# Fifty-three weight chunks of a float32 decoder block brought in and split by two GpSimd DMAs each, with the low-part matmuls moved behind the high-part ones

## The chip, the cores and the metric

The kernel runs on one core of one Trainium2 chip. The metric is the device time of one execution in microseconds. The trace is one profiled execution; times in it count from the start of its span. TensorE's clock has two levels, 1.2 and 2.4 GHz, and the profile shows the granted one as a share of the higher.

## What is computed

One decoder layer on 512 tokens of 1024 columns, in float32. The reference, cut to what matters here:

```python
h = rms_norm(x, g_norm1) * (1.0 + sc1) + sh1
z = h @ w_in                       # 8 kinds of columns, split below
(gu, gv, mq, mk, mv, mo, mi, mf, nq, nkc, nvc, nks, nvs, nkw, nvw, ngate, ga, gbr, gc) = split(z)
y_a = gmlp_mixer(gu, gv, ...) @ w_up_a
y_b = mlstm_mixer(mq, mk, mv, mo, mi, mf, ...) @ w_up_b
y_c = nsa_mixer(nq, nkc, nvc, nks, nvs, nkw, nvw, ngate, ...) @ w_up_c
x = x + gt1 * ((sigmoid(ga) * y_a + sigmoid(gbr) * y_b + sigmoid(gc) * y_c) @ w_out)
h = rms_norm(x, g_norm2) * (1.0 + sc2) + sh2
x = x + gt2 * (square(relu(h @ w_mlp1)) @ w_mlp2)
return rms_norm(x, g_final)
```

`sh1`, `sc1` and the other four rows of the modulation come from `silu(c) @ w_ada + b_ada`.

## The kernel before

Float32 products are made of float32r parts: a value is a high part (rounded to float32r) plus a low part (the rest), and each product takes three matmuls: high with high, low activations with high weights, high activations with low weights (`mm3`). The activations h^T stay in SBUF as eight pairs `hh[k]`, `hl[k]`. The weights come in chunks of 128 x 1024 (some 768, 864 or 576 columns wide). For each chunk, `chunk()` does three things: SyncE loads a tile `w_raw` (three buffers), ScalarE copies it rounded into `w_hi`, and an engine subtracts: `w_lo = w_raw - w_hi`. `w_hi` and `w_lo` have two buffers each, so chunk n+2 takes the tiles of chunk n. With `pool_lo=True` GpSimd does the subtraction, otherwise VectorE. GpSimd has 53 chunks: 8 of `w_early` (the first GEMM, six column tiles of q and k, one chunk for each block k), 2 of `w_zt` (compressed keys and values), 3 of `w_small`, 12 in `early_fill` (beside the attention loop), 24 in the gated merges of branches 2 and 0, and 4 in `fill_og`. The chunks of the conv, of merge 1 and of everything after them are VectorE's.

The stages in order of time: a start that loads x and makes the norm and the modulation of the first sub-layer (`early_mod`, `early_h`: VectorE and GpSimd multiply the transposed rows of `w_ada` by the condition, tile `ada_raw`, line L207 on GpSimd and L210 on VectorE), with the first GEMM running along it, one chunk per block; the two `zt` tiles and the three `sm` chunks; the attention loop with `early_fill` between its steps; the merges with the conv and the mLSTM heads; then the rest of the modulation, the output projection and the MLP.

What sets the order: each engine runs its own instructions in program order and waits there. In the first GEMM the order on TensorE is as written, in the attention loop that on TensorE, ScalarE and VectorE is; elsewhere, and always on GpSimd and on SyncE's DMA queue, a scheduler fixes the order when the program is built. The loop of the first GEMM, the same in both kernels, is this (c0 to c7 below are its eight chunks):

```python
            for i in range(6):
                T.matmul(early[i], wh[:, tsl(i)], hh[j], start=j == 0, stop=False)
            ...
            for i in range(6):
                T.matmul(early[i], wh[:, tsl(i)], hl[j], start=False, stop=False)
                T.matmul(early[i], wl[:, tsl(i)], hh[j], start=False, stop=j == KD - 1)
```

The functions that the change touches:

Of the kernel before, what the change touches and what calls it, by code (L numbers as in the profile page):

```python
# [11 lines left out]
ALU = mybir.AluOpType  # L12
# [48 lines left out]
def trunk_kernel(ctx: ExitStack, tc: tile.TileContext, x, vecs, rows, late_rows, ada1, w_ada,  # L61
# [15 lines left out]
    def page(tag, name, dt=F32, width=S):  # L77
        """a tile of 512 columns (and a little) that outlives the step that writes it"""
        t = work.tile([P, 520 if tag == "kv" else S], dt, name=name, tag=tag, bufs=SLOTS[tag])
        return t[:, :width]  # L80
# [10 lines left out]
    def split(hi, lo, src, scale=None):  # L91
        """src (times scale) as the exact sum of two float32r parts"""
        if scale is None:
            A.copy(hi, src)
            V.tensor_tensor(lo, src, f(hi), op=ALU.subtract)
        else:
            A.activation(hi, src, AF.Copy, scale=scale)
            V.scalar_tensor_tensor(lo, src, scale, f(hi), op0=ALU.mult, op1=ALU.subtract)
# [6 lines left out]
    def chunk(src, cols=D, pool_lo=False, dve_hi=False):  # L105
        raw = load(src, cols)
        hi = stream.tile([P, D], F32R, name="w_hi", tag="hi")[:, :cols]
        lo = stream.tile([P, D], F32R, name="w_lo", tag="lo")[:, :cols]
        V.tensor_copy(hi, raw) if dve_hi else A.copy(hi, raw)  # L109
        (G if pool_lo else V).tensor_tensor(lo, raw, f(hi), op=ALU.subtract)  # L110
        return hi, lo
# [5 lines left out]

    def rstd_of(ss, n, name, scale=1.0 / D):
        """1/sqrt(ss*scale + EPS)"""
        r = small.tile([P, n], F32, name=name)  # L120
        V.tensor_scalar(r, ss, scale, EPS, op0=ALU.mult, op1=ALU.add)
        G.tensor_tensor(r, r, mhalf[:, 0:r.shape[1]], op=ALU.pow)
        return r
# [4 lines left out]
    # ---------------------------------------------------------------- loads and constants of the start  # L128
# [24 lines left out]
    # the condition as a row on all partitions  # L153
# [7 lines left out]
    # ---------------------------------------------------------------- first norm, transposed and split  # L161
# [20 lines left out]
    # 1/rms of the tokens as a row on all partitions  # L182
# [9 lines left out]
    def early_mod(j):  # L192
        """shift and scale of a column tile: the first by the tensor engine, the others along rows of the
        transposed weights"""
# [61 lines left out]
    # ---------------------------------------------------------------- constants of the mixers  # L256
# [23 lines left out]
    # ---------------------------------------------------------------- GEMM helpers on h^T  # L280
    def zt(n, pool_lo=False, tag="mm"):
        """column tile n of z, transposed: [128 columns, S]"""
        wh, wl = chunk(w_zt[n], D, pool_lo)
        ps = bank(tag, "zt")
        for k in range(KD):
            mm3(ps, wh[:, tsl(k)], wl[:, tsl(k)], hh[k], hl[k], k == 0, k == KD - 1)
        return ps

    def ztok(n, evac, pool_lo=True):
        """256 columns of z in token layout: two banks of two blocks; a step for each chunk of weights"""  # L290
        ps = [bank("mm", "ztok") for _ in range(2)]
        for c in range(2):
            wh, wl = chunk(w_tok[n * 2 + c], D, pool_lo)
            for tb in range(NT):
                o = ps[tb // 2][:, (tb % 2) * 256:(tb % 2) * 256 + 256]
                for kk in range(4):
                    k = 4 * c + kk
                    ws_ = slice(kk * 256, (kk + 1) * 256)
                    T.matmul(o, hh[k][:, tsl(tb)], wh[:, ws_], start=k == 0 and tb % 2 == 0, stop=False)
                    T.matmul(o, hl[k][:, tsl(tb)], wh[:, ws_], start=False, stop=False)  # L300
                    T.matmul(o, hh[k][:, tsl(tb)], wl[:, ws_], start=False, stop=k == KD - 1 and tb % 2 == 1)
# [6 lines left out]
    # ---------------------------------------------------------------- NSA operands  # L308
# [32 lines left out]
    # compressed keys and values: the windows, gathered by pairs of positions  # L341
    vc = []
    # per group: 32 columns of the high parts, 32 of the low ones
# [20 lines left out]
    def halves(name, src, eng):  # L364
        """16 blocks of 64 columns, each beside its rest: both float32r parts in one operand of 128 columns"""
# [42 lines left out]
    # values of the two dense branches, mLSTM gates, NSA gates: token layout  # L408
# [6 lines left out]
    for c, (k0, k1) in enumerate(((0, 3), (3, 6), (6, 8))):  # L415
        wh, wl = chunk(w_small[:, k0 * 288:k1 * 288], (k1 - k0) * 288, pool_lo=True)
        for tb in range(NT):
            for k in range(k0, k1):
                ws_ = slice((k - k0) * 288, (k - k0 + 1) * 288)
                T.matmul(sm[tb][:, :288], hh[k][:, tsl(tb)], wh[:, ws_], start=k == 0, stop=False)  # L420
                T.matmul(sm[tb][:, :288], hl[k][:, tsl(tb)], wh[:, ws_], start=False, stop=False)
                T.matmul(sm[tb][:, :288], hh[k][:, tsl(tb)], wl[:, ws_], start=False, stop=k == KD - 1)
# [11 lines left out]
    # ---------------------------------------------------------------- NSA attention  # L434
# [4 lines left out]
    def cmp_scores(g):  # L439
        """scores and weights of the compressed branch for the four heads of group g, in steps"""  # L440
# [43 lines left out]
    def scores(n, tb):  # L484
        """a block of rows of the scores, their bias and their maximum"""
# [24 lines left out]
    def scale(n, t0, t1):  # L510
        """exp(s - max) of blocks t0 to t1 times gate / sum"""
# [10 lines left out]
    def turn(n, sb):  # L522
        """the weights of a block of keys, transposed"""
# [14 lines left out]
    def apply(n, sb):  # L538
        """values of a block of keys times their weights"""
# [32 lines left out]
    # ---------------------------------------------------------------- gMLP  # L572
# [12 lines left out]
    def gelu2(ts):  # L585
        """twice the gelu, in place"""
# [54 lines left out]
    def mlstm_gates():  # L641
# [23 lines left out]
        # sums of the log forget gates within blocks of 128, the running stabilizer  # L665
# [37 lines left out]
    def evac_mv(half):  # L703
        def ev(tb, ps):
            # two heads to a page: high part, one, zero, low part
# [14 lines left out]
    def conv(i, ps):  # L720
        """column tile i of q and k after the conv, silu and scale: two float32r parts"""
# [99 lines left out]
    # ---------------------------------------------------------------- merge of the gated branches  # L821
# [3 lines left out]
    def merge(b, yh, yl):  # L825
        """adds branch b of the three, two column tiles at a time: gates, then the projection up"""
        for jp in range(4):
# [8 lines left out]
            wh, wl = chunk(w_up[b][jp], D, pool_lo)  # L836
            for u in range(2):
                j = 2 * jp + u
                ps = bank(UP_BANK[b][u], "up")
                for k in range(4):  # L840
                    mm3(ps, wh[:, tsl(u * 4 + k)], wl[:, tsl(u * 4 + k)], yh[k], yl[k], k == 0, k == 3)
# [12 lines left out]
    # ---------------------------------------------------------------- mixers beside the GEMMs  # L854
    def early_fill():
        """the first GEMMs on h^T in small steps, with the weights of the next chunk under way"""
# [7 lines left out]
        for m, (kind, i) in enumerate(units):  # L864
# [3 lines left out]
            if kind == "z":  # L868
                ps = bank("mm", "zt")
                for k in range(KD):  # L870
                    mm3(ps, wh[:, tsl(k)], wl[:, tsl(k)], hh[k], hl[k], k == 0, k == KD - 1)
                    if k < KD - 1:
# [8 lines left out]
            for tb in range(NT):  # L881
                o = ps[tb // 2][:, (tb % 2) * 256:(tb % 2) * 256 + 256]
                for kk in range(4):
                    k = 4 * c + kk
                    ws_ = slice(kk * 256, (kk + 1) * 256)
                    T.matmul(o, hh[k][:, tsl(tb)], wh[:, ws_], start=k == 0 and tb % 2 == 0, stop=False)  # L886
                    T.matmul(o, hl[k][:, tsl(tb)], wh[:, ws_], start=False, stop=False)  # L887
                    T.matmul(o, hh[k][:, tsl(tb)], wl[:, ws_], start=False, stop=k == KD - 1 and tb % 2 == 1)
                    if kk == 1 or (kk == 3 and (c == 0 or tb % 2 == 0)):
                        yield  # L890
                if c == 1 and tb % 2 == 1:
                    ev = (evac_gv(0), evac_gv(1), evac_mv(0), evac_mv(1))[n]
                    for t_ in (tb - 1, tb):
                        ev(t_, ps[t_ // 2][:, (t_ % 2) * 256:(t_ % 2) * 256 + 256])
                    yield
# [68 lines left out]
    # row sums of the masked weights carry the bias of the norm  # L964
# [38 lines left out]
    # ---------------------------------------------------------------- the rest of the modulation  # L1003
# [58 lines left out]
    # ---------------------------------------------------------------- output projection, second norm  # L1062
# [14 lines left out]
    def tok_gemm(chunks, ah, al, finish, tags, held=None, between=None, tail=None):  # L1077
        """sum over k of ah/al[k]^T times two blocks of weight rows per chunk, in token layout; with pages for the
        last chunks (held) the blocks finish one after the other"""
# [17 lines left out]
        def half_step(u, k, wh, wl):  # L1097
            """the last block of tokens, half of the columns"""
# [108 lines left out]
    # ---------------------------------------------------------------- MLP  # L1207
# [15 lines left out]
    def final_half(ps, u, us):  # L1223
        """the last block, half of its last columns at a time"""
# [24 lines left out]
    def relu2(n, ps):  # L1249
        """relu squared, split"""  # L1250
# [32 lines left out]
def _layout(inp):  # L1283
# [7 lines left out]
    def tiles_t(w):  # L1291
        """[K, N] -> [N/128, 128, K] : column tile, row in its block, (block, column)"""
# [3 lines left out]
    def tiles_k(w):  # L1296
        """[K, N] -> [N/512 * K/256, 128, 1024] : half, pair of row blocks"""
# [60 lines left out]
```

## Time and profile before

| What | Value |
|---|---|
| Times of three runs | 972.73, 973.5, 974.67 us (median 973.5) |
| Span of the profiled execution | 973.2 us |
| TensorE busy | 933.4 us, 96% |
| VectorE busy | 612.2 us, 63% |
| ScalarE busy | 402.4 us, 41% |
| GpSimd busy | 193.7 us, 20% |
| DMA | 111.72 MB, 115 GB/s on average |

The profiled execution has no time apart from its span; the span lies 0.3 us under the median. TensorE's busy time counts overlapping matmuls once, and a matmul of 512 columns that shows 0.39 us of its own starts 0.23 us after the one before it, so "busy" does not mean that no faster pace is possible, but idle time of TensorE is real idle time.

### The profile page before, as it was taken

The numbers are of one execution on the slowest core, as the hardware profiler recorded it, in microseconds if no ns is written. First come the engines' busy times: TensorE is split into PE (matmuls) and PEld (weight loads), VectorE is DVE, ScalarE is ACT, GpSimd is POOL, SyncE is SP. The second block draws the span as 40 slices with busy tenths as digits, with TensorE's granted clock in tenths as the row PEclk, the third lists the DMA queues.
The fourth block names the chain that finished last, engine by engine and source line by source line (L and its number), as shares of the span: only waits on it lengthen the run. The fifth ranks groups of instructions, "written<-read, shape, count | busy, mean of one in ns | idle before, by whom it ended". The sixth has DMA issues, their size and how long they took to land.

```text
span 973.2 us, 12531 instructions
## 1 busy us (share of the span) xinstructions
PE 933.4 (96%) x4688; PEld 778.5 (80%) x4688; DVE 612.2 (63%) x1186; ACT 402.4 (41%) x789; POOL 193.7 (20%) x130
## 2 busy tenths in 40 slices
PE   7789998998979999999999999999999999999996
PEld 5569986797867888888977778888888888888886
DVE  6977679776497456556688799766424254442435
ACT  5355565765533444443333344544321223432221
POOL 5565423333343122123300003000000000000001
PEclk9899999998999999999999999999999999999998
DMA  9733210110222222222568864354333333223222
GB/s 328 229 118 116 66 44 26 40 44 26 84 65 87 87 86 88 70 82 89 172 211 274 258 251 119 92 182 128 94 100 91 104 89 107 87 89 106 87 87 87
DMA packets 36285, 111.72 MB, mean 115 GB/s; under 512 B 4160, under 2 KB 4352, under 8 KB 36224
## 3 DMA queue, kind: packets, MB, share of 16 engines
q1 hardware_dynamic: 36224, 110.91, 35.0%
q8 instruction: 37, 0.61, 0.3%
q14 instruction: 24, 0.20, 0.1%
HBM read 108.80 MB, written 2.10 MB: 114 GB/s over the span
## 4 chain that ended last, share of the span: by engine, by line
PE 75%; DVE 15%; DMA 6%; issue 2%; ACT 1%; SPq 0%; POOL 0%; POOLq 0%; DVEq 0%; ACTq 0%
PE tok L1086 6%; PE tok L1088 6%; PE tok L1087 6%; PE m L114 6%; PE m L116 6%; PE m L115 6%; PE zt L116 5%; PE zt L114 5%; PE zt L115 5%; DMA ada_raw<-in_w_ada 4%; DVE ada_raw L210 2%; PE pv L553 2%; PE pT L528 2%; PE ztok L887 2%; PE ztok L886 2%
## 5 line engine op out<-in xcount | busy, mean ns | idle before, releaser
L109 ACT CAST w_hi<-w_raw 128x1024 fp32r<-128x1024 f32 (+2 forms) x137 | 141.4, 1032 | 256.6 <-PE tok L1087 98.0
L110 DVE TENSOR_TENSOR w_lo<-w_raw,w_hi 128x1024 fp32r<-128x1024 f32 x84 | 103.8, 1236 | 171.1 <-ACT w_hi L109 171.1
L110 POOL TENSOR_TENSOR w_lo<-w_raw,w_hi 128x1024 fp32r<-128x1024 f32 (+3 forms) x53 | 125.1, 2360 | 242.9 <-ACT w_hi L109 240.3
L116 PE MATMUL zt<-h_hi,w_lo 128*128 128x512 f32 x304 | 121.1, 398 | 4.0 <-POOL w_lo L110 2.3
L114 PE MATMUL zt<-h_hi,w_hi 128*128 128x512 f32 x304 | 122.3, 402 | 0.5 <-ACT w_hi L109 0.5
L115 PE MATMUL zt<-h_lo,w_hi 128*128 128x512 f32 x304 | 119.9, 394 | 0.0
L114 PE MATMUL m<-h_hi,w_hi 128*128 128x512 f32 (+1 forms) x272 | 104.1, 383 | 0.0
L116 PE MATMUL m<-h_hi,w_lo 128*128 128x512 f32 (+1 forms) x272 | 103.7, 381 | 0.0
L115 PE MATMUL m<-h_lo,w_hi 128*128 128x512 f32 (+1 forms) x272 | 103.6, 381 | 0.0
L1087 PE MATMUL tok<-w_hi,f_lo 128*128 128x512 f32 (+1 forms) x232 | 88.6, 382 | 0.0
L1086 PE MATMUL tok<-w_hi,f_hi 128*128 128x512 f32 (+1 forms) x232 | 88.6, 382 | 0.0
L1088 PE MATMUL tok<-w_lo,f_hi 128*128 128x512 f32 (+1 forms) x232 | 84.4, 382 | 0.0
L116 PEld LDWEIGHTS zt<-h_hi,w_lo 128*128 128x128 f32 x304 | 57.6, 190 | 17.3 <-DVE w_lo L110 2.8
L114 PEld LDWEIGHTS zt<-h_hi,w_hi 128*128 128x128 f32 x304 | 57.6, 189 | 12.1 <-ACT w_hi L109 0.7
L115 PEld LDWEIGHTS zt<-h_lo,w_hi 128*128 128x128 f32 x304 | 57.6, 190 | 10.7
L1228 POOL TENSOR_TENSOR o_g<-x,gfin 128x512 f32<-128x512 f32 x1 | 1.3, 1297 | 311.0 <-DVE x L1132 311.0
L115 PEld LDWEIGHTS m<-h_lo,w_hi 128*128 128x128 f32 x272 | 51.2, 188 | 10.8
L116 PEld LDWEIGHTS m<-h_hi,w_lo 128*128 128x128 f32 x272 | 51.1, 188 | 10.8
L114 PEld LDWEIGHTS m<-h_hi,w_hi 128*128 128x128 f32 x272 | 51.1, 188 | 10.7
L1087 PEld LDWEIGHTS tok<-w_hi,f_lo 128*128 128x128 f32 x232 | 43.6, 188 | 8.6
L1086 PEld LDWEIGHTS tok<-w_hi,f_hi 128*128 128x128 f32 x232 | 43.6, 188 | 8.5
L1088 PEld LDWEIGHTS tok<-w_lo,f_hi 128*128 128x128 f32 x232 | 43.6, 188 | 8.4
(390 smaller groups left out, 2022.3 us busy)
## 6 DMA issues: line engine op xcount, KB each, us to landing
w_raw<-in_w_m SPq DMA_DIRECT2D x64, 512.0 KB, 3.5
w_raw<-in_w_zt SPq DMA_DIRECT2D x38, 512.0 KB, 3.3
ada_raw<-in_w_ada SPq DMA_DIRECT2D x24, 512.0 KB, 5.1
ada_raw<-in_ada SPq DMA_DIRECT2D x32, 256.0 KB, 4.9
w_raw<-in_w_tok SPq DMA_DIRECT2D x12, 512.0 KB, 3.3
w_raw<-in_w_up SPq DMA_DIRECT2D x12, 512.0 KB, 3.5
w_raw<-in_w_out SPq DMA_DIRECT2D x8, 512.0 KB, 4.8
w_raw<-in_w_ada SPq DMA_DIRECT2D x8, 512.0 KB, 3.9
```

The lines of the kernel that those rows point to most:

```text
L109: V.tensor_copy(hi, raw) if dve_hi else A.copy(hi, raw)
L110: (G if pool_lo else V).tensor_tensor(lo, raw, f(hi), op=ALU.subtract)
L114: T.matmul(ps, ah, bh, start=first, stop=False)
L115: T.matmul(ps, ah, bl, start=False, stop=False)
L116: T.matmul(ps, al, bh, start=False, stop=last)
L210: V.scalar_tensor_tensor(raws[q], raws[q], 1.0, condb[:, (q % 2) * 512:(q % 2) * 512 + 512], op0=ALU.mult, op1=ALU.mult, accum_out=s4[:, q ...
L528: T.transpose(tp[:, tsl(tb)], sb_[:, boff(tb) + c0:boff(tb) + c0 + P], ident)
L553: T.matmul(acc[:, c0:], vv, p_[:, c0:], start=False, stop=last and p_ is t[-1])
L886: T.matmul(o, hh[k][:, tsl(tb)], wh[:, ws_], start=k == 0 and tb % 2 == 0, stop=False)
L1086: T.matmul(p_, ah_, wh, start=k == 0, stop=False)
L1087: T.matmul(p_, al_, wh, start=False, stop=False)
L1088: T.matmul(p_, ah_, wl, start=False, stop=k == 2 * n - 1)
```

## The change

For the 53 chunks with `pool_lo`, `w_raw`, ScalarE's copy and GpSimd's subtraction go. GpSimd issues a DMA from HBM straight into `w_hi`, which rounds on the way. ScalarE writes the negative of `w_hi` into `w_lo`. GpSimd then issues a second DMA of the same weights, which adds them to `w_lo`. Outside the first GEMM the matmuls that read `w_lo` move behind all that read `w_hi` of the same chunk. The core of the diff:

```diff
     def chunk(src, cols=D, pool_lo=False, dve_hi=False):
-        raw = load(src, cols)
         hi = stream.tile([P, D], F32R, name="w_hi", tag="hi")[:, :cols]
         lo = stream.tile([P, D], F32R, name="w_lo", tag="lo")[:, :cols]
+        if pool_lo:
+            G.dma_start(hi, src)
+            A.activation(lo, f(hi), AF.Copy, scale=-1.0)
+            G.dma_start(lo, src, accum_op=ALU.add)
+            return hi, lo
+        raw = load(src, cols)
         V.tensor_copy(hi, raw) if dve_hi else A.copy(hi, raw)
-        (G if pool_lo else V).tensor_tensor(lo, raw, f(hi), op=ALU.subtract)
+        V.tensor_tensor(lo, raw, f(hi), op=ALU.subtract)
         return hi, lo
...
+    def mm_hi(ps, ah, bh, bl, first):
+        T.matmul(ps, ah, bh, start=first, stop=False)
+        T.matmul(ps, ah, bl, start=False, stop=False)
...
         for k in range(KD):
-            mm3(ps, wh[:, tsl(k)], wl[:, tsl(k)], hh[k], hl[k], k == 0, k == KD - 1)
+            mm_hi(ps, wh[:, tsl(k)], hh[k], hl[k], k == 0)
+        for k in range(KD):
+            T.matmul(ps, wl[:, tsl(k)], hh[k], start=False, stop=k == KD - 1)
...
```

`ztok`, the `sm` loop, `early_fill` and the projections up in `merge` are split in the same way (16 or 32 matmuls on the high tile, then 8 or 16 on the low one); `merge` opens both of its two banks before the first low matmul.

In the rows that follow, line numbers are those of each kernel's own file. GpSimd's queue, in the first GEMM, before. `w_lo_268` is the low tile of c1, `w_lo_317` of c2, and so on; the `ada_raw` rows are the modulation's:

```order
L207 TENSOR_TENSOR ada_raw_259<-ada_raw_259,condb_119 128x512
L110 TENSOR_TENSOR w_lo_268<-w_raw_265,w_hi_267 128x768
L207 TENSOR_TENSOR ada_raw_308<-ada_raw_308,condb_119 128x512
L110 TENSOR_TENSOR w_lo_317<-w_raw_314,w_hi_316 128x768
L207 TENSOR_TENSOR ada_raw_357<-ada_raw_357,condb_119 128x512
L110 TENSOR_TENSOR w_lo_366<-w_raw_363,w_hi_365 128x768
```

The same queue after the change. `w_hi_312` and `w_lo_313` belong to c2, 360 and 361 to c3, 408 and 409 to c4, 456 to c5:

```order
L110 DMA w_hi_312<-in_w_early 128x768
L218 TENSOR_TENSOR ada_raw_354<-ada_raw_354,condb_119 128x512
L110 DMA w_hi_360<-in_w_early 128x768
L218 TENSOR_TENSOR ada_raw_402<-ada_raw_402,condb_119 128x512
L112 DMA w_lo_313<-in_w_early 128x768
L218 TENSOR_TENSOR ada_raw_450<-ada_raw_450,condb_119 128x512
L112 DMA w_lo_361<-in_w_early 128x768
L218 TENSOR_TENSOR ada_raw_498<-ada_raw_498,condb_119 128x512
L218 TENSOR_TENSOR ada_raw_546<-ada_raw_546,condb_119 128x512
L110 DMA w_hi_408<-in_w_early 128x768
L112 DMA w_lo_409<-in_w_early 128x768
L110 DMA w_hi_456<-in_w_early 128x768
```

The subtractions are gone, each chunk has two DMA issues in their place, and the low DMA of c2 stands behind the high DMA of c3, that of c4 ahead of the high DMA of c5.

TensorE's order where the two `zt` tiles meet, before (tile `zt_701`, then `zt_745`; three kinds of matmul in turn):

```order
L116 MATMUL zt_701<-h_hi_534,w_lo_698 128x512
L114 MATMUL zt_701<-h_hi_583,w_hi_697 128x512
L115 MATMUL zt_701<-h_lo_584,w_hi_697 128x512
L116 MATMUL zt_701<-h_hi_583,w_lo_698 128x512
L114 MATMUL zt_745<-h_hi_246,w_hi_741 128x512
L115 MATMUL zt_745<-h_lo_247,w_hi_741 128x512
```

And after the change (the tiles are `zt_692` and `zt_735` here):

```order
L126 MATMUL zt_735<-h_hi_527,w_hi_730 128x512
L127 MATMUL zt_735<-h_lo_528,w_hi_730 128x512
L126 MATMUL zt_735<-h_hi_575,w_hi_730 128x512
L127 MATMUL zt_735<-h_lo_576,w_hi_730 128x512
L299 MATMUL zt_692<-h_hi_245,w_lo_688 128x512
L299 MATMUL zt_692<-h_hi_287,w_lo_688 128x512
L299 MATMUL zt_692<-h_hi_335,w_lo_688 128x512
```

The eight low matmuls of the first tile now stand behind all high ones of the second; those of the second stand inside the first `sm` chunk.

## Rows read from the trace of the kernel before

**Rows 1.** The page, busy time of each engine (share of the span).
```profile
PE 933.4 (96%) x4688; PEld 778.5 (80%) x4688; DVE 612.2 (63%) x1186; ACT 402.4 (41%) x789; POOL 193.7 (20%) x130
```

**Rows 2.** Windows: stretch, length, busy time per engine (count), granted clock, DMA share, GB/s.
```profile
8.00:18.00 10.00, 9.85 (x58) 7.38 (x56) 6.03 (x19) 5.07 (x11) 2.86 (x2) 0.90 1.01 385
...
35.00:68.00 33.00, 27.58 (x110) 21.01 (x109) 28.59 (x47) 13.19 (x23) 20.53 (x13) 0.95 0.50 165
68.00:96.00 28.00, 27.98 (x182) 25.71 (x181) 20.78 (x49) 17.37 (x31) 16.43 (x9) 1.00 0.42 131
...
106.00:258.00 152.00, 144.47 (x906) 125.63 (x906) 108.07 (x334) 92.71 (x252) 49.37 (x31) 0.98 0.13 42
258.00:300.00 42.00, 36.80 (x160) 28.77 (x158) 40.51 (x63) 20.79 (x34) 17.35 (x9) 0.92 0.28 89
300.00:457.00 157.00, 157.00 (x748) 130.47 (x748) 90.66 (x160) 65.80 (x129) 41.33 (x17) 1.00 0.25 81
```

**Rows 3.** TensorE's waits, 0 to 70 us and 100 to 300 us (total, times, longest).
```profile
PE early L249 <- ACT h_hi L232: 7.9, 4, 4.8
...
PE pT L528 <- DVE scores L518: 7.3, 8, 2.4
PE zt L116 <- POOL w_lo L110: 2.3, 1, 2.3
```

**Rows 4.** Timeline of VectorE: start, length, line, operation.
```profile
21.55 2.32 DVE L210 SCALAR_TENSOR_TENSOR ada_raw<-ada_raw,condb 128x512 f32<-128x512 f32 x1
...
25.36 1.94 DVE L231 SCALAR_TENSOR_TENSOR h_tmp<-xT,ab,rb 128x512 f32<-128x512 f32 x1
...
28.91 0.68 DVE L210 SCALAR_TENSOR_TENSOR ada_raw<-ada_raw,condb 128x512 f32<-128x512 f32 x1
...
31.29 0.75 DVE L231 SCALAR_TENSOR_TENSOR h_tmp<-xT,ab,rb 128x512 f32<-128x512 f32 x1
...
222.74 2.13 DVE L503 TENSOR_SCALAR mx<-mx 128x4 f32<-128x4 f32 x1
```

**Rows 5.** Timeline of GpSimd at the same moments, then two groups by shape.
```profile
21.04 2.29 POOL L110 TENSOR_TENSOR w_lo<-w_raw,w_hi 128x768 fp32r<-128x768 f32 x1
...
24.96 1.80 POOL L110 TENSOR_TENSOR w_lo<-w_raw,w_hi 128x768 fp32r<-128x768 f32 x1
...
222.45 2.39 POOL L110 TENSOR_TENSOR w_lo<-w_raw,w_hi 128x1024 fp32r<-128x1024 f32 x1 [11.89 <-ACT w_hi L109]
...
L110 POOL TENSOR_TENSOR w_lo<-w_raw,w_hi 128x1024 fp32r<-128x1024 f32 x42 | 103.3, 2460 | 214.8 <-ACT w_hi L109 212.3 <-issue 2.4
L207 POOL TENSOR_TENSOR ada_raw<-ada_raw,condb 128x512 f32<-128x512 f32 x7 | 11.7, 1672 | 2.9 <-ACT condb L243 2.9
```

**Rows 6.** Timeline of TensorE in the first GEMM.
```profile
28.11 2.92 PE L249 MATMUL early<-h_hi,w_hi 128*128 128x512 f32 x6 [4.76 <-ACT h_hi L232]
...
31.27 0.63 PE L254 MATMUL early<-h_hi,w_lo 128*128 128x512 f32 x1
31.69 0.63 PE L253 MATMUL early<-h_lo,w_hi 128*128 128x512 f32 x1
...
34.62 1.52 PE L249 MATMUL early<-h_hi,w_hi 128*128 128x512 f32 x6
...
67.41 0.39 PE L254 MATMUL early<-h_hi,w_lo 128*128 128x512 f32 x1
67.64 0.39 PE L114 MATMUL zt<-h_hi,w_hi 128*128 128x512 f32 x1
```

**Rows 7.** DMA issues: KB each, median us to landing; whole span, last row 20 to 60 us.
```profile
w_raw<-in_w_zt SPq DMA_DIRECT2D x38, 512.0 KB, 3.3
...
w_raw<-in_w_small SPq DMA_DIRECT2D x1, 288.0 KB, 2.7
...
w_raw<-in_w_early SPq DMA_DIRECT2D x4, 384.0 KB, 4.0
```

**Rows 8.** Groups of ScalarE by shape: busy, mean ns; then one issue on SyncE's timeline.
```profile
L109 ACT CAST w_hi<-w_raw 128x1024 fp32r<-128x1024 f32 x126 | 132.3, 1050 | 249.2 <-PE tok L1087 98.0 <-PE m L115 66.5 <-PE zt L115 39.1
...
L109 ACT CAST w_hi<-w_raw 128x768 fp32r<-128x768 f32 x8 | 6.6, 830 | 7.3 <-DMA w_raw<-in_w_early 2.5 <-DMA ada_raw<-in_ada 2.3 <-issue 1.4
...
318.49 0.33 SPq L102 DMA_DIRECT2D w_raw<-in_w_up  x1
```

More of the change, by code (lines that the diff above doesn't have):

```diff
@@ L293, in ztok @@
             wh, wl = chunk(w_tok[n * 2 + c], D, pool_lo)
-            for tb in range(NT):
+            for tb, kk in [(tb, kk) for tb in range(NT) for kk in range(4)]:
                 o = ps[tb // 2][:, (tb % 2) * 256:(tb % 2) * 256 + 256]
[L296 to L301, printed above, removed]
+                k = 4 * c + kk
+                ws_ = slice(kk * 256, (kk + 1) * 256)
+                T.matmul(o, hh[k][:, tsl(tb)], wh[:, ws_], start=k == 0 and tb % 2 == 0, stop=False)
+                T.matmul(o, hl[k][:, tsl(tb)], wh[:, ws_], start=False, stop=False)
+            for tb, kk in [(tb, kk) for tb in range(NT) for kk in range(4)]:
+                o = ps[tb // 2][:, (tb % 2) * 256:(tb % 2) * 256 + 256]
+                k = 4 * c + kk
+                T.matmul(o, hh[k][:, tsl(tb)], wl[:, kk * 256:(kk + 1) * 256], start=False,
+                         stop=k == KD - 1 and tb % 2 == 1)
             if c == 0:
@@ L421, in trunk_kernel @@
                 T.matmul(sm[tb][:, :288], hl[k][:, tsl(tb)], wh[:, ws_], start=False, stop=False)
+        for tb in range(NT):
+            for k in range(k0, k1):
+                ws_ = slice((k - k0) * 288, (k - k0 + 1) * 288)
                 T.matmul(sm[tb][:, :288], hh[k][:, tsl(tb)], wl[:, ws_], start=False, stop=k == KD - 1)
@@ L836, in merge @@
             wh, wl = chunk(w_up[b][jp], D, pool_lo)
+            ups = [bank(UP_BANK[b][u], "up") for u in range(2)]
+            for u in range(2):
+                for k in range(4):
+                    mm_hi(ups[u], wh[:, tsl(u * 4 + k)], yh[k], yl[k], k == 0)
             for u in range(2):
                 j = 2 * jp + u
-                ps = bank(UP_BANK[b][u], "up")
+                ps = ups[u]
                 for k in range(4):
-                    mm3(ps, wh[:, tsl(u * 4 + k)], wl[:, tsl(u * 4 + k)], yh[k], yl[k], k == 0, k == 3)
+                    T.matmul(ps, wl[:, tsl(u * 4 + k)], yh[k], start=False, stop=k == 3)
                 if macc[j] is None:
@@ L869, in early_fill @@
                 ps = bank("mm", "zt")
-                for k in range(KD):
-                    mm3(ps, wh[:, tsl(k)], wl[:, tsl(k)], hh[k], hl[k], k == 0, k == KD - 1)
-                    if k < KD - 1:
+                mms = [(wh, k, o) for k in range(KD) for o in (hh, hl)] + [(wl, k, hh) for k in range(KD)]
+                for n_, (w_, k, o) in enumerate(mms):
+                    T.matmul(ps, w_[:, tsl(k)], o[k], start=n_ == 0, stop=n_ == len(mms) - 1)
+                    if n_ % 3 == 2 and n_ < len(mms) - 1:
                         yield
@@ L880, in early_fill @@
                 ps = [bank("mm", "ztok") for _ in range(2)]
-            for tb in range(NT):
+            mms = [(tb, kk, a_, wh) for tb in range(NT) for kk in range(4) for a_ in (hh, hl)]
+            mms += [(tb, kk, hh, wl) for tb in range(NT) for kk in range(4)]
+            for n_, (tb, kk, a_, w_) in enumerate(mms):
+                k = 4 * c + kk
                 o = ps[tb // 2][:, (tb % 2) * 256:(tb % 2) * 256 + 256]
[L883 to L891, printed above, removed]
+                T.matmul(o, a_[k][:, tsl(tb)], w_[:, kk * 256:(kk + 1) * 256],
+                         start=k == 0 and tb % 2 == 0 and a_ is hh and w_ is wh,
+                         stop=k == KD - 1 and tb % 2 == 1 and w_ is wl)
+                if c == 1 and w_ is wl and kk == 3 and tb % 2 == 1:
                     ev = (evac_gv(0), evac_gv(1), evac_mv(0), evac_mv(1))[n]
@@ L894, in early_fill @@
                         ev(t_, ps[t_ // 2][:, (t_ % 2) * 256:(t_ % 2) * 256 + 256])
+                if n_ % 6 == 5:
                     yield
```

## The prediction

> **What bounds the kernel now.** I read the page's busy times first, then windows by stage, then TensorE's waits, then the timelines at those waits. TensorE is busy for 96% [rows 1], so a change to the feeding of weights can win back at most the idle 4%, 40 us, and can lose without such a bound. The windows say where there is something to win: TensorE idles 5.4 us of 33 in the first GEMM (35 to 68 us), 7.5 us of 152 in the attention loop, 5.2 us of 42 at the first merge, and nothing in the zt and sm stage (68 to 96) or between 300 and 457 us [rows 2]. What it waits for there is not weights but VectorE: 7.9 us for `h_hi`, which ScalarE makes from VectorE's `h_tmp`, and 7.3 us for the softmax scales of line 518. One wait of 2.3 us is for GpSimd's `w_lo` itself [rows 3].
>
> VectorE is late partly because of GpSimd. The same `ada_raw` multiply takes 0.68 us alone and 2.32 us at 21.55, `h_tmp` 0.75 and 1.94 us, and a negation of four columns takes 2.13 us at 222.74 [rows 4]. Each time GpSimd is in a `w_lo` subtraction that began just before, at 21.04, 24.96 and 222.45, and VectorE goes on when it ends [rows 5]. The subtractions, 2.46 us each at 1024 columns [rows 5], go with the change, so this delay goes.
>
> **Prices of what is added.** ScalarE's negation has the shape of the copy that it replaces, 1.05 us, or 0.83 at 768 columns [rows 8]: nothing as work, but it now stands between two transfers. No row shows a DMA issued by GpSimd or one that adds. Issue: at least SyncE's 0.33 us [rows 8], at most GpSimd's longest plain row in this stage, the 1.67 us multiply [rows 5]; I take 0.5, near SyncE's, since both only write out a transfer. High load: 384 KB land after 4.0 us in this stage, 512 KB after 3.3 on a free queue [rows 7]. So high = 4.5 in the first GEMM (4.0 + 0.5), 3.8 later. Low load: below, the same, if reading `w_lo` back is free; above, twice the landing. 288 KB take 2.7 and 512 KB 3.3 us [rows 7], so each further 224 KB cost 0.6 and a second pass over the chunk 1.0 us (384 KB) or 1.4 (512 KB). I take that: low = 5.5 in the first GEMM, 5.2 later. The Trainium skill gives 2.0 us plus the bytes at 436 GB/s for a GpSimd DMA (DMA: Bandwidth & Descriptors, Anatomy of one DMA — SWDGE (gpsimd) path), an estimate of 2.9 us for 384 KB, against 4.0 in the row for SyncE's DMA in this stage; with 2.9 for both loads the first GEMM would end some 5 us earlier than before and the sum come to about 964. No run here shows such a DMA yet.
>
> **First GEMM.** Before, three `w_raw` buffers were filled ahead. Now c(n+2) cannot even start to load until TensorE is through with c(n), and its way is long: high load, negation (0.9 with its wait), low load, then the 11 of 18 matmuls that stand from the first low one on. These start 0.23 us apart (67.41 and 67.64 [rows 6]): 2.5 us.
> c1 ends at 34.6 before [rows 6]. Two locks on its way vanish, 1.6 and 1.2 us [rows 4]; two high chunks, 0.79 MB, now pass ahead of the modulation's first weights at 385 GB/s [rows 2], 2.0 us. So c1 ends at 34.
> c2's low DMA stands behind c3's high one, which waits for the end of c1: 34 + 0.5 + 5.5 + 2.5 = 42.5.
> c4 waits for the end of c2: 42.5 + 4.5 + 0.9 + 5.5 + 2.5 = 55.9.
> c5's high DMA stands behind c4's low one and leaves at 48.4, its low one at 53.8: end 61.8.
> c6 starts to load at 55.9, its low DMA leaves at 61.3: end 69.3.
> c7 loads from 61.8 on: 61.8 + 5.4 + 5.5 + 2.5 = 75.2. Before, 67.64 [rows 6]: **+7.6**.
> c3, whose low tile is asked for at 35.5, fits between. VectorE, which before was just ahead of each chunk, loses its locks and is no limit here.
> Clock: after the idle 4.76 us before 28.11, matmuls started 0.43 us apart instead of 0.23 (31.27 and 31.69 [rows 6]), the lower level. In the new chain TensorE stands for 4.4, 4.8 and 3.4 us before the low matmuls of c2, c4 and c6. I charge two of the three with 11 x 0.2 us: **+4.4**.
> Bounds, the chain with 0.3, 3.6 and 3.6 us: end 66.4, -1.2, no clock. With 1.7, 5.7 and 9.7: end 93.8, +26, and all three clocks, +6.6.
>
> **zt and sm chunks.** The new order of matmuls gives low loads time: the second tile's high matmuls (16 x 0.23 = 3.7 us) run before the first low one. With 3.8 and 5.2, one wait of 2.0 us remains, at the first sm chunk, whose tile is free only after the first zt tile's low matmuls, and one of 0.2: **+2.2**, since this stage has no idle time before (0 to +8).
>
> **Attention loop.** A chunk of `early_fill` lasts at least 12.7 us here (152 us [rows 2] for the 12 of them), so two chunks hide the whole way of a load. The high tile is free after two thirds, 4.2 us before the chunk ends, and ScalarE, whose order is fixed, comes to the negation about when the 3.8 us load lands: no cost. Of the 7.3 us that TensorE waited for scales [rows 3], the lock at 222.74 was worth 2.0; I take **-3** (0 to -7.3).
>
> **Merges.** First merge, 258 to 300 us: VectorE is busy 40.5 of 42 us [rows 2], the 2.3 us wait for GpSimd's tile goes; -3 for locks, +2 for loads that start late: **-1** (-5.2 to +2). From 300 to 457 us TensorE is never idle. A chunk of 24 matmuls lasts 24 x 0.23 = 5.5 us. GpSimd's chain per chunk, where high and low DMA alternate, is 3.8 + 1.05 + 0.5 = 5.35 us: it just holds. From free high tile to full low tile are 3.8 + 1.05 + 5.2 + 0.5 = 10.6 us, where two chunks give 11: it just holds. I take **+2** for ScalarE's other work in the way.
>
> **Sum.** 7.6 + 4.4 + 2.2 - 3 - 1 + 2 = +12.2, on the span of 973.2: 985.4; the median lies 0.3 above that span: 986 us. The likeliest case's own range is 979 to 994, chance 0.48.
>
> **The rivals.**
> *Faster.* The locks decide and the loads are as short as SyncE's: -1.2 in the first GEMM, nothing at zt and sm, the full -7.3 and -5.2 later: 960 at best. It decides from c7's end before some 72 us on, that is, with high and low load both near 4 us and no lower clock. For it speak [rows 4, 5]; against it that a DMA that adds must read two streams. About 966, chance 0.25.
> *The adding DMA is expensive.* With 1.7, 5.0 and 8.3 us GpSimd's chain is 5.0 + 1.05 + 1.7 = 7.75 us per chunk against 6.2 that the 32 chunks (24 of GpSimd's, 8 of the conv) from 258 to 457 us now take on average (199 / 32): up to 1.55 x 24 = 37 us in the merges alone. Half of that, with half of the upper bound in the first GEMM (16) and 3 behind it: some 1010. Chance 0.15.
> *The issue is slowed by VectorE,* a lock the other way round: in the merges each of 48 issues waits 0.35 us, half a VectorE pass of 0.7 us like those in [rows 4]; GpSimd's chain becomes 6.05 us, above 5.5, 0.55 x 24 = 13 us, half of it hidden beside the heads' matmuls: 986 + 6 = 992. The Trainium skill states that lock (SBUF — State Buffer, SBUF: two separate sides, on descriptors that GpSimd cannot write while VectorE runs a 2-port pass); no run here shows it yet. Chance 0.07.
> *No change,* locks and loads equal: chance 0.05.
>
> A difference within 0.2%, 2 us, can't be told from none. Faster is 0.25, same 0.05, slower 0.48 + 0.15 + 0.07 = 0.70. The range runs from 962 to 1016 and leaves out the best end of the first rival and the worst of the second.
>
> **What would show it.** In the changed profile: c7 ends near 75 to 80 us and TensorE waits there for DMAs, not for `h_hi`; low DMAs land after 5 to 6 us; `ada_raw` multiplies at 0.68 us except where GpSimd's own multiply runs; the granted clock below 0.9 from 35 to 75 us; the waits on line 518's counterpart shorter; 300 to 457 us within 3 us of its length. Wrong if low DMAs land in under 4 us (then faster) or in over 8 (then far slower), or if ScalarE's negation, waiting for its load, holds up the softmax.

## The result and the profile after

The changed kernel takes 1019.6 us (median of 4 runs, 1014.0 to 1024.0) beside 973.5 us for the kernel before on the same chip: ratio 1.045, 95% interval 1.042 to 1.048 (the two medians alone give 1.047). The forecast was 986 us, 962 to 1016: the sign was right, the size a quarter of what came.

The page's busy times and DMA queues (packets, MB, share of 16 engines' span) of the changed kernel, answering to [rows 1]:

```profile
PE 944.6 (93%) x4688; PEld 786.2 (77%) x4688; DVE 568.7 (56%) x1186; ACT 405.0 (40%) x789; POOL 142.9 (14%) x183
...
q1 hardware_dynamic: 28592, 84.56, 25.3%
q0 software_dynamic: 15264, 52.70, 23.8%
```

VectorE is busy 43 us less, GpSimd 51 us. TensorE idles 74.5 us where it idled 39.8, and is busy 11.2 us longer, since more of its matmuls run at the lower clock (windows below): together the 45.9 us by which the span grew. GpSimd's queue (q0) moves 38% of the bytes in nearly half of the packet time.

TensorE's waits of the changed kernel (total, times, longest), answering to [rows 3]:

```profile
PE early L265 <- DMA w_lo<-in_w_early: 19.9, 5, 8.1
PE zt L299 <- DMA w_lo<-in_w_zt: 7.4, 6, 1.9
PE ztok L316 <- DMA w_lo<-in_w_tok: 6.4, 3, 3.7
PE x_T L180 <- DMA x_in<-in_x: 5.8, 3, 4.6
PE sm L441 <- DMA w_lo<-in_w_small: 4.6, 2, 2.8
PE up L126 <- ACT sig L852: 4.4, 1, 4.4
...
PE early L260 <- ACT h_hi L243: 2.1, 1, 2.1
PE pT L547 <- DVE scores L537: 2.1, 5, 0.8
PE up L864 <- DMA w_lo<-in_w_up: 2.0, 2, 1.8
```

The waits for `h_hi` and for the softmax scales fell from 7.9 and 7.3 us to 2.1 and 2.1; one of 4.4 us for ScalarE's `sig` is new. TensorE now waits 19.9 + 7.4 + 6.4 + 4.6 + 2.0 = 40.3 us for low loads; before, it waited 4.6 us for low tiles.

Why they come late is in the two lines of `chunk()`. First the adding DMA, line 112 (what GpSimd idled for before it, then the time from issue to landing), then the high one, line 110:

```profile
  ACT w_lo L111: 174.4, 38
...
DMA to landing us min/median/max: 4.4/5.4/8.5
```

```profile
  ACT w_lo L111: 91.3, 32
...
DMA to landing us min/median/max: 3.1/4.7/8.9
```

GpSimd stood 174 us ahead of 38 low issues until ScalarE had negated; ScalarE stood 91 us for high loads. Such a stand holds up whatever is behind it in GpSimd's queue, but it costs time only where TensorE runs out of work: in a kernel below whose second DMA only writes, GpSimd stood 167.6 us ahead of the same 38 issues, and the loss was a third of this one.

The stages, as delays of the changed kernel behind the one before (start of the same matmul in both timelines):

| Point | Before | After | Delay | Gained or lost since | Forecast of that step |
|---|---|---|---|---|---|
| last matmul of c7 | 67.4 | 91.5 | +24.1 | +24.1 | +12.0 |
| last `sm` matmul | 95.5 | 127.3 | +31.8 | +7.7 | +2.2 |
| last `pv` (end of the attention loop) | 256.4 | 284.8 | +28.4 | -3.4 | -3 |
| third pair of merge 2 | 310.1 | 334.0 | +23.8 | -4.5 | -1 |
| middle of the last pair of merge 0 | 454.8 | 490.4 | +35.7 | +11.8 | +2 |
| last matmul of `fill_og` | 484.6 | 532.2 | +47.6 | +12.0 | 0 |
| first `tok` matmul | 560.1 | 602.3 | +42.1 | -5.5 | 0 |
| end | 973.2 | 1019.1 | +45.9 | +3.8 | 0 |

Two windows, answering to [rows 2] (same columns):

```profile
35.00:68.00 33.00, 20.02 (x67) 15.18 (x66) 24.10 (x57) 12.25 (x20) 15.79 (x15) 0.78 0.75 206
68.00:96.00 28.00, 19.92 (x71) 14.87 (x69) 3.44 (x5) 5.59 (x8) 5.00 (x8) 0.88 0.52 120
```

The clock is at 0.78 and 0.88 where it was 0.95 and 1.00. TensorE's and GpSimd's timelines show one link of the chain, c5 to c7:

```profile
77.34 0.40 PE L265 MATMUL early<-h_hi,w_lo 128*128 128x512 f32 x1
...
87.67 0.80 PE L265 MATMUL early<-h_hi,w_lo 128*128 128x512 f32 x1 [3.02 <-DMA w_lo<-in_w_early]
...
88.69 0.63 PE L265 MATMUL early<-h_hi,w_lo 128*128 128x512 f32 x1
...
91.51 0.40 PE L265 MATMUL early<-h_hi,w_lo 128*128 128x512 f32 x1
```

```profile
77.81 0.56 POOL L110 DMA_DIRECT2D w_hi<-in_w_early  x1 [1.45 <-PE early L265]
82.72 0.86 POOL L112 DMA_DIRECT2D w_lo<-in_w_early  x1 [4.36 <-ACT w_lo L111]
```

c5's last matmul frees the tiles, the high load goes out at 77.81, the low one 4.9 us later, the first low matmul runs another 5.0 us later, and the 11 matmuls from there take 4.1 us, most of them 0.85 us a pair at the lower clock level. That is 14.2 us for a link that the prediction had at 13.4 without the clock: the high load with its negation and the low load were some 0.5 us shorter each than forecast, the matmuls 1.6 us longer.

### The profile page after: what moved, and what is told of

Same layout as the page of the kernel before. It is cut to its first block, busy times and chain, and to the rows that moved or that the text cites. A ratio compares the mean times of both kernels' runs of the same rounds, so it can differ in the third digit from the quotient of the medians.

```text
span 1019.1 us, 12571 instructions
## 1 busy us (share of the span) xinstructions
PE 944.6 (93%) x4688; PEld 786.2 (77%) x4688; DVE 568.7 (56%) x1186; ACT 405.0 (40%) x789; POOL 142.9 (14%) x183
## 3 DMA queue, kind: packets, MB, share of 16 engines
q0 software_dynamic: 15264, 52.70, 23.8%
## 4 chain that ended last, share of the span: by engine, by line
PE 71%; issue 10%; DMA 9%; DVE 6%; POOL 2%; ACT 2%; SPq 0%; POOLq 0%; ACTq 0%; DVEq 0%
PE tok L1110 6%; PE tok L1112 6%; PE tok L1111 6%; PE m L121 6%; PE m L120 6%; PE m L122 6%; PE zt L299 5%; PE zt L126 5%; PE zt L127 5%; PE ztok L911 3%; DMA w_lo<-in_w_zt 2%; PE pv L572 2%; DMA ada_raw<-in_ada 2%; PE zt L895 2%; PE up L864 2%
## 5 line engine op out<-in xcount | busy, mean ns | idle before, releaser
L115 ACT CAST w_hi<-w_raw 128x1024 fp32r<-128x1024 f32 x84 | 88.2, 1050 | 205.4 <-PE tok L1111 97.4
L126 PE MATMUL zt<-h_hi,w_hi 128*128 128x512 f32 x272 | 107.6, 396 | 1.3 <-DMA w_hi<-in_w_zt 1.3
L127 PE MATMUL zt<-h_lo,w_hi 128*128 128x512 f32 x272 | 106.6, 392 | 0.0
L111 ACT ACTIVATE w_lo<-w_hi 128x1024 fp32r<-128x1024 f32 (+3 forms) x53 | 53.8, 1015 | 105.4 <-DMA w_hi<-in_w_zt 32.5
L299 PE MATMUL zt<-h_hi,w_lo 128*128 128x512 f32 x272 | 70.6, 397 | 7.4 <-DMA w_lo<-in_w_zt 7.4
L299 PEld LDWEIGHTS zt<-h_hi,w_lo 128*128 128x128 f32 x272 | 50.0, 188 | 19.5 <-DMA w_lo<-in_w_zt 9.5
L126 PEld LDWEIGHTS zt<-h_hi,w_hi 128*128 128x128 f32 x272 | 51.1, 188 | 13.1 <-issue 1.5
L121 PEld LDWEIGHTS m<-h_lo,w_hi 128*128 128x128 f32 x272 | 51.1, 188 | 10.6
L122 PEld LDWEIGHTS m<-h_hi,w_lo 128*128 128x128 f32 x272 | 51.1, 188 | 10.6
L127 PEld LDWEIGHTS zt<-h_lo,w_hi 128*128 128x128 f32 x272 | 51.1, 188 | 10.3
```

The source lines that it names most:

```text
L111: A.activation(lo, f(hi), AF.Copy, scale=-1.0)
L121: T.matmul(ps, ah, bl, start=False, stop=False)
L122: T.matmul(ps, al, bh, start=False, stop=last)
L126: T.matmul(ps, ah, bh, start=first, stop=False)
L127: T.matmul(ps, ah, bl, start=False, stop=False)
L299: T.matmul(ps, wl[:, tsl(k)], hh[k], start=False, stop=k == KD - 1)
```

## The experiments

Theory A: the way of a chunk is a series (high load, negation, adding load) that begins when one of two tiles is free and goes through GpSimd's queue in order, and it is too long for TensorE's chunk. Theory B: the transfers themselves, twice the reads by a slower queue, are too dear. Theory C: the new order of matmuls costs.

**Where the loss lies: the first GEMM on the old way, the four `fill_og` chunks on the old way, the first GEMM alone on the new way.** The edit of the first two is a condition in `chunk()`, by the place of the call ('e' the first GEMM, 'o' `fill_og`), here in short; the third is the kernel before with the two DMAs written out for `w_early` alone:

```diff
-        if pool_lo:
+        if pool_lo and pool_lo != 'e':        # second kernel: != 'o'
             G.dma_start(hi, src)
...
-        V.tensor_tensor(lo, raw, f(hi), op=ALU.subtract)
+        (G if pool_lo else V).tensor_tensor(lo, raw, f(hi), op=ALU.subtract)
```

> The 8 chunks of the first GEMM go back to the old way (SyncE load, ScalarE copy, GpSimd subtraction); the other 45 keep the two DMAs. Theory A (a serial way per chunk, high load, then ScalarE's negation, then the adding load, that can begin only when a tile of the two buffers is free): the first GEMM again ends near 67 to 69 us instead of 91.5, and the time falls by 20 to 25 us, to 995 to 1000. Theory B (the doubled reads and the slow queue burden all of the kernel): as the traffic elsewhere stays, the later stages are as late as in the changed kernel; B allows the same fall, so this run places the loss and does not choose between A and B. If the 46 us are mostly elsewhere (the new order of matmuls, theory C), the time stays above 1010.

Measured: 999.8 us, ratio to the kernel before 1.026 (1.023 to 1.028). c7 ends 0.7 us behind the kernel before; 19 (by the ratios) to 20 us are won back, a little short of the 20 to 25 expected.

> The changed kernel with the 4 chunks of the stage after the conv (fill_og) back on the old way. There the changed kernel lost 12 us, of which 5.5 were given back in the merge behind it. Theory A: the stage again takes 27 us and not 39, and the time falls by 5 to 10 us, to 1010 to 1015. If VectorE's work on the merge and the rest of the modulation, and not the tokens' GEMM, ends that stretch: less than 3 us, above 1016.

Measured: 1006.3 us, ratio 1.035 (1.030 to 1.040), so 10 (by the ratios) to 13 us won, more than expected: the stage has its 27 us again, and the 5.5 us that the changed kernel won in the merge behind it are won here too (they come with the new order: the kernel with the order alone, below, wins them as well).

> The kernel before, with only the 8 chunks of the first GEMM by two DMAs; all else, the order of the matmuls too, as before. If the loss of the first GEMM is its own (theory A; putting it back in the changed kernel gave 20 us): the first GEMM ends near 90 us, the time is 991 to 998. If it needs the traffic or the order of the other chunks (the tiles of zt and sm asked for ahead): under 988.

Measured: 992.2 us, ratio 1.016 (1.013 to 1.020). Its TensorE waits show the same row as the changed kernel, 17.3 us for `w_lo` (19.9 there). So the first GEMM's loss is its own; alone it costs 16 to 20 us.

**The order alone.** All chunks by the old way, matmuls in the new order.

> All 53 chunks by the old way (SyncE load, ScalarE copy, GpSimd subtraction), only the matmuls in the new order, low part last. Theories A and B: within 4 us of the kernel before, 970 to 977. Theory C (the order itself costs, since a high tile is held while the next one's matmuls run and low tiles come free later): 982 or more, with the loss in the sm, merge and og stages.

Measured: 973.4 us, ratio 0.998 (0.997 to 1.000). The new order costs nothing in the sum (the attention loop ends 7.8 us later, and later stages give it back). Theory C falls.

**More tiles in the first GEMM.** Every third chunk takes two of the `w_raw` buffers:

```diff
-        ws_early[j] = chunk(w_early[j], 768, pool_lo=True)
+        ws_early[j] = chunk(w_early[j], 768, pool_lo=True, tags=("raw", "raw") if j % 3 == 2 else ("hi", "lo"))
```

> The changed kernel with a third pair of tiles for every third chunk of the first GEMM (the raw buffers, idle there). Theory A with the two buffers as the cause: a chunk's way of some 13 us can begin one chunk earlier, so that c7 ends near 80 instead of 91.5 us and the time falls by 8 to 14 us, to 1006 to 1012. If it is GpSimd's queue in order, in which a low DMA holds up the next high one, that sets the pace whatever the buffers: less than 4 us gained, above 1015. Theory B (transfers): no gain either, with longer landings.

Measured: 1013.9 us, ratio 1.040 (1.037 to 1.043): 5 to 6 us won, between the two expectations. c7 ended at 80.8, as theory A had it, but the `zt` and `sm` chunks behind it lost 10.6 instead of 7.7 us. Buffers are a part of it.

**What of the way costs: series and adding.** Four kernels with the same loads and bytes, the changed one among them; the other three leave the whole weights in the low tile and serve for timing alone. Two things are switched: whether ScalarE writes the negative of the high tile (so the low load waits for the high one) or zeros (so it does not), and whether the second DMA adds or only writes. The edits, each against the changed kernel:

```diff
             G.dma_start(hi, src)
-            A.activation(lo, f(hi), AF.Copy, scale=-1.0)                            # zeros:
+            A.activation(lo, ones[:, 0:1].to_broadcast([P, cols]), AF.Copy, scale=0.0)
-            G.dma_start(lo, src, accum_op=ALU.add)                                  # only writes:
+            G.dma_start(lo, src)
```

> The changed kernel, but ScalarE writes zeros instead of the negative of the high tile, so that the adding DMA waits for the low tile and for ScalarE alone, not for the high load; the low tile then holds the whole weights. Same DMAs, same bytes, same ScalarE work. Theory A (the serial way): the first GEMM gains 12 to 20 of its 24 us, zt and sm and og most of their 20, the time falls to 980 to 992. Theory B (price of the transfers and of the queue): stays at 1010 or above.

> The changed kernel with a second DMA that does not add: it writes the weights into the low tile, ScalarE's negation is left out (the low tile holds the whole weights), and it waits for a free tile alone. Beside the run with zeros in place of the negative (995.1 us; low loads of 512 KB landed there after 5.4 to 5.5 us, high ones after 3.7 to 4.4) it differs by the reading back. If the adding is what makes the second load dear, low loads land like the high ones, near 4 us, and the time falls by a further 5 to 12 us, to 983 to 990. If it is the queue and the second reading of the weights from HBM (theory B), low loads stay above 5 us and the time within 4 us of 995.

> As the run with zeros in place of the negative (995.1 us, adding DMA), but the second DMA only writes: ScalarE's zeros and the waits stay, the reading back goes; the low tile holds the whole weights. It parts the 19 us by which the run without ScalarE's write and without adding (976.2 us) is shorter. If the adding is the price: 975 to 981, low loads near 4.5 us. If ScalarE's place in the way of the low load is: 990 to 995, low loads near 4.5 us all the same.

> The changed kernel with its whole way in series (high load, ScalarE's negation, second load), but the second DMA only writes; the low tile holds the whole weights. The prices, if they add: the series costs some 20 to 24 us over a kernel with two free loads (976.2 us), the adding the same over one without it, so 995 to 1003. If adding and series need each other (each alone is hidden): 980 to 990. If the series is all: 1012 or more.

Measured, as medians and as ratios to the kernel before on the same chip:

| | second DMA only writes | second DMA adds |
|---|---|---|
| zeros: loads apart | 976.8 us, 1.004 (1.002 to 1.006) | 995.1 us, 1.020 (1.017 to 1.023) |
| negative: loads in series | 986.7 us, 1.015 (1.011 to 1.018) | 1019.6 us, 1.045 (1.042 to 1.048) |

Without ScalarE's write at all and without adding: 976.2 us, 1.001 (0.999 to 1.003), so ScalarE's write costs 0.3% at most; 976.2 us lies below both cases that were expected of it. By the ratios series alone costs 1.1%, adding alone 1.6%, both 4.2%: more than the sum by 1.5%, some 14 us. So neither theory has it alone: without the series 980 to 992 was expected by A and 1010 or more by B. The last two kernels came where their first and second case said: the adding is the price of the second load, not ScalarE's place in its way, and series and adding together cost more than each by itself.

The two switches are not equally clean. Between adding and only writing, the traces show the same order of matmuls and of GpSimd's issues. Between negative and zeros the scheduler also changed both orders, so "series" here means the wait with the order that comes with it: in the two kernels in series 15 of the 42 high loads of 512 KB leave within 1.3 us behind a low load, in those with zeros 2 (adding) and 3 (writing).

What adding does stands in the landing times from issue, line 112. The three kernels in turn: negative and only writing, zeros and adding, zeros and only writing.

```profile
DMA to landing us min/median/max: 3.3/3.6/6.8
```

```profile
DMA to landing us min/median/max: 4.6/5.5/10.1
```

```profile
DMA to landing us min/median/max: 3.3/3.6/7.7
```

And in the queue of GpSimd (kernel with zeros and adding, then with zeros and only writing), for the same bytes:

```profile
q0 software_dynamic: 15264, 52.70, 24.3%
```

```profile
q0 software_dynamic: 15264, 52.70, 17.5%
```

An adding load lands 1.8 to 1.9 us later. The packets took 24.3% of 993.6 us against 17.5% of 974.9, 241 against 171 us of 16 engines: with half of the bytes each, an adding byte costs (241 - 85) / 85 = 1.8 times a plain one.

Where the two together cost more than the sum can be read stage by stage, as in the table of the result, in the order zeros and writing, zeros and adding, negative and writing, negative and adding. The first GEMM ends 6.6, 14.7, 16.0 and 24.1 us behind the kernel before: there the prices simply add. `fill_og` loses 0.0, 0.5, 1.5 and 12.0 us: some 10 of the 14 us beyond the sum arise there. In this stage the high load of a chunk is issued right behind the low load of the chunk before. DMA issues of 493 to 523 us in the changed kernel, then of 458 to 490 us (the same stage) in that with the negative and only writing:

```profile
w_lo<-in_w_tok POOLq DMA_DIRECT2D x4, 512.0 KB, 5.4
w_hi<-in_w_tok POOLq DMA_DIRECT2D x3, 512.0 KB, 7.4
```

```profile
w_hi<-in_w_tok POOLq DMA_DIRECT2D x4, 512.0 KB, 5.3
w_lo<-in_w_tok POOLq DMA_DIRECT2D x4, 512.0 KB, 3.6
```

Not only the low load is slower, the high one beside it is too, by 2.1 us, and the high one is what the next negation waits for. The whole traces say the same of more loads: the 15 high loads right behind a low one land after 6.4 us at the median in the changed kernel (5.6 to 8.9) and after 4.9 in that with the negative and only writing (4.1 to 6.5), those more than 3 us behind one after 3.75 and 3.65 (24 loads each). GpSimd's row in this stage of the changed kernel:

```profile
494.41 0.86 POOL L110 DMA_DIRECT2D w_hi<-in_w_tok  x1
503.24 0.86 POOL L112 DMA_DIRECT2D w_lo<-in_w_tok  x1 [7.97 <-ACT w_lo L111]
503.79 0.87 POOL L110 DMA_DIRECT2D w_hi<-in_w_tok  x1
511.77 0.85 POOL L112 DMA_DIRECT2D w_lo<-in_w_tok  x1 [7.11 <-ACT p_hi L94]
512.32 0.87 POOL L110 DMA_DIRECT2D w_hi<-in_w_tok  x1
522.61 0.85 POOL L112 DMA_DIRECT2D w_lo<-in_w_tok  x1 [9.43 <-ACT num_lo L793]
```

The stage took 27.1 us for its 4 chunks before, 6.8 us for each with the matmuls of a head between them; from low issue to low issue GpSimd takes 8.5 to 10.8. In the kernel with the negative that only writes it takes 7.2 to 8.4, and the stage loses 1.5 us instead of 12. That the slower high load is what takes the loop beyond the length that TensorE hides is read from these rows. No kernel was run in which only the place of the high load, away from the adding one, was changed.

**The new way where two chunks' time hides it.** The DMAs only in the 12 chunks of `early_fill`; then also in the 12 of merge 2; then the first with the order of the kernel before everywhere outside `early_fill`.

> The two DMAs only in the 12 chunks beside the attention loop, the other 41 by the old way, all matmuls in the new order. Theory A: here two chunks' time covers a chunk's way, and GpSimd's subtractions, which hold VectorE up, are gone: the loop, 6.6 us longer in the run with the new order alone (973.4 us) and 3.4 us shorter in the changed kernel, wins 7 to 10 us of which some is lost to later waits: 964 to 970. If the loop's end is not what sets the merges (VectorE is), or the loads hurt here too: 972 or more.

Measured: 969.8 us, ratio 0.994 (0.992 to 0.996).

> As the run before it in this list, and the 12 chunks of the merge of branch 2 by two DMAs as well. The changed kernel won 4.5 us between the end of the attention loop and the second pair of that merge and lost some 7 from there to the end of it: within 4 us of the run with the attention loop alone if gain and loss cancel; theory A expects a loss of 2 to 6 us where merge chunks follow each other every 5.5 us, faster than GpSimd's row of high load, negation and two issues of some 7 us; theory B (price of transfers alone) no loss, since the DMA engines are under 60 per cent busy there.

Measured: 972.0 us, ratio 0.996 (0.994 to 0.997). Theory A expected a loss of 2 to 6 us against the run before it; the 2.2 us measured are within the spread of the two and do not tell.

> The two DMAs and the new order only in the 12 chunks beside the attention loop, everything else as in the kernel before. With the new order everywhere this gave 969.8 us. If the new order elsewhere neither helps nor hurts: within 2 us of that, 968 to 972. If it helped there (the run with the order alone won 10 us between the first merge and the last): 974 to 978.

Measured: 965.6 us, ratio 0.991 (0.988 to 0.995), faster than both kernels and 2.4 us below the lower bound of its first case. The new order outside `early_fill` did not help. TensorE's waits and the DMA issues of this version:

```profile
PE pT L534 <- DVE scores L524: 1.2, 4, 0.4
PE ztok L894 <- DMA w_lo<-in_w_tok: 0.9, 1, 0.9
```

```profile
w_hi<-in_w_tok POOLq DMA_DIRECT2D x8, 512.0 KB, 3.6
w_lo<-in_w_tok POOLq DMA_DIRECT2D x8, 512.0 KB, 5.4
```

The adding load is as slow as anywhere, and TensorE waits 0.9 us for it; the wait for the softmax scales went from 7.3 [rows 3] to 1.2 us. With the new order alone it is 7.5 us, so it is the DMAs that take it away.

## Why the prediction was wrong, step by step

- **The mechanism** (high load, negation, adding load in a row, started only when a tile is free) was right: TensorE waits for low loads, 40.3 us in all, and hardly for `h_hi`. Prices were wrong, in the first GEMM and in the merges, and `fill_og` was left at nothing. None of the prediction's own signs of being wrong came: low loads landed neither under 4 us nor, at the median, over 8, and the waits for the softmax scales fell.
- **The first GEMM, +12.0 with the clock, measured +24.1: the main step that failed.** The price of a link was nearly right (14.2 against 13.4 us from c5 to c7). What failed is the start of the chain and the sum of small things in it. c1 ended at 37.8 and not at 34: TensorE began c0 6.2 us late, at 24.8. The prediction charged 2.0 us for the two high chunks that pass ahead at the start and nothing for the two low ones, which pass there too. The loads of x, beside which they now pass, landed after 6.2 us (5.1 before, 4.6 with the first GEMM on the old way), the first `ada_raw` loads after 7.7 (5.5 before); TensorE waited 2.1 us for `ada_raw`, before not at all. How the 6.2 us are made up was not followed further. Where the low DMAs only write, in series, c0 began 3.9 us late, so some 2.3 us go with the adding: from 11 to 16 us, while the two adding loads ran, the DMA engines moved 263 GB/s, against 408 before and 398 where they only write. c2 ended at 52.3 and not at 42.5. Its low DMA stood behind GpSimd's own `ada_raw` multiply of 1.3 us as well as c3's high issue (the order shown ahead of the prediction has that row between them), and landed after 7.8 us and not 5.5 (median of the two adding loads issued from 38 to 50 us, beside eight loads of `ada_raw`):

```profile
38.88 1.29 POOL L218 TENSOR_TENSOR ada_raw<-ada_raw,condb 128x512 f32<-128x512 f32 x1
40.11 0.95 POOL L112 DMA_DIRECT2D w_lo<-in_w_early  x1
...
47.89 0.80 PE L265 MATMUL early<-h_hi,w_lo 128*128 128x512 f32 x1 [8.11 <-DMA w_lo<-in_w_early]
```

  c4's high load stood behind a multiply that had waited for its `ada_raw`, and left 1.6 us after the last matmul of c2. c5's low load landed after 7.0 us. The clock fell before c2, c4, c5 and c7, and each time the matmuls behind took up to 0.85 us a pair, some 7 us in all over 0.23 us each: the charge of two such falls (4.4 us) was too low. (The 35.5 at which the prediction lets c3's low tile be asked for doesn't follow from its own prices, 34 + 4.5 + 0.9 = 39.4; its sum does not use it.)
- **zt and sm, +2.2, measured +7.7.** The mechanism is that of the step, its price was too low: the high loads of 432 KB landed after 5.4 us, not 3.8, and the waits for `w_small` were 4.6 us.
- **The attention loop, -3, measured -3.4,** and the lock that it stood on is gone. VectorE's groups of the changed kernel, by shape:

```profile
L221 DVE SCALAR_TENSOR_TENSOR ada_raw<-ada_raw,condb 128x512 f32<-128x512 f32 x21 | 16.4, 809 | 0.0
...
L522 DVE TENSOR_SCALAR mx<-mx 128x4 f32<-128x4 f32 x16 | 3.1, 194 | 0.6
```

  The 16 `mx` take 3.1 us, where they took 5.1 before with the one of 2.13 in [rows 4]; `ada_raw` has a mean of 0.81 us, before 1.20. Rows of 1.8 to 2.3 us are left where GpSimd's own multiply runs, as forecast. That the number fits is in part luck: the prediction puts the new order at nothing in this stage, and in the kernel with the order alone the stage is 6.6 us longer, so the DMAs won more than 3.
- **First merge -1, measured -4.5:** why is not shown. The order alone wins 1.7 us of it; that the locks were worth more and the late loads less is argued.
- **Merges +2, measured +11.8, and `fill_og` 0, measured +12.0: the second step that failed.** The prediction had GpSimd's loop at 3.8 + 1.05 + 0.5 = 5.35 us, "it just holds" against 5.5. Its terms measured: high landing 6.4 us right behind an adding load and 7.4 in `fill_og`, negation 1.06, and 0.55 from the low issue to the high one behind it; at 370 us it is 8.4 us from low issue to low issue. The step that failed is thus the high landing, taken at 3.8 us, which is near that of a free queue (3.3). The low landing, 5.4 us, was as forecast (5.2). A loop that only just holds was charged +2; its upper bound went into a rival alone, at half, and `fill_og`, 4 chunks in the same pattern, was put at nothing without a reason. Adding without the series costs the merges 8.4 us too, in another order of matmuls, with one wait of 4.3 us for a low load; that loss is not this loop's, and its cause stays open.
- **The rivals.** "Faster" fails: low loads do not land in 4 us. "The adding DMA is expensive" is nearest (1010), and its point, a loop longer than TensorE's chunk, is what decides; but its low load of 8.3 us is not needed, since the slower high load behind it does the same. "The issue is slowed by VectorE" fails: the longest of 106 issues lasted 1.18 us, and issues of DMAs that only write 0.53 us at the median. The Trainium skill's lock of GpSimd's descriptors by VectorE (SBUF — State Buffer, SBUF: two separate sides) is thus not seen in these issues.
- The Trainium skill's 2.0 us plus bytes at 436 GB/s (DMA: Bandwidth & Descriptors, Anatomy of one DMA — SWDGE (gpsimd) path) gives an estimate of 3.2 us for 512 KB. DMAs that only write came near it, 3.6 us from issue to landing; adding ones took 5.4. By it the loop would hold, as it does with two plain loads in series: that kernel loses 0.4 us in the merges and 1.5 in `fill_og`.

## What to carry to other kernels

Before work is moved from an engine into DMAs, write down the loop of the queue that issues them (each landing that it waits for, each issue) and set it against the time that TensorE needs for a chunk. Take the landing of a load as it is beside the other loads of the loop, not on a free queue. Where the margin is small (here 0.15 of 5.5 us), price the loop at its upper bound in every stage that has it; `fill_og` lost 12 us over 4 chunks. The adding DMAs paid in the one place where two chunks of other work lay between issue and use: there they took VectorE's stalls away, and 12 of the 53 chunks gave 0.9% while all 53 cost 4.5%. In the 12 chunks of merge 2 the runs show neither gain nor loss.

## What the runs showed of the hardware

- A DMA of 512 KB from GpSimd that adds to a float32r tile landed after 5.4 us, one that only writes after 3.6, and per byte it took 1.8 times the DMA engines' packet time.
- Its issue shows 0.86 us at the median against 0.53 us for one that only writes. GpSimd is not held for that long: its next instruction can start 0.55 us after the issue began (503.24 and 503.79 above), hardly later than the 0.51 to 0.52 behind one that only writes.
- A rounding load of 512 KB issued within 1.3 us behind an adding load landed after 6.4 us at the median, behind one that only writes after 4.9 (15 loads each), and after 3.7 to 3.8 with no low load in the 3 us before it.
- While two adding loads of 384 KB ran beside other loads (11 to 16 us), the DMA engines moved 263 GB/s, against 398 with two that only write.
